# Hybrid encoder block on one core: GpSimd's share of the full stages given to VectorE, and VectorE and ScalarE ordered by due time

## The chip, the core and the metric

The kernel runs on one core of a Trainium2 chip. Five engines work side by side: PE (TensorE, matrix products), DVE (VectorE), ACT (ScalarE), POOL (GpSimd) and SP (SyncE, which here issues most DMAs). Each engine takes its own instructions in the order in which the program gives them to it, and waits on semaphores for the others. The metric is the device time of one launch in microseconds (us), lower is better.

## What is computed

One layer of an encoder with batch 1, 512 positions and width 1024, all in float32:

```
mod = silu(c) @ w_ada + b_ada                       # six vectors: shift, scale, gate for two sub-layers
h   = rms_norm(x, norm1_g) * (1 + sc1) + sh1
xr, yr, q, k, v, gates = split(h @ w_in)
branch_a = (bidir_rg_lru(depthwise_conv(xr)) * gelu(yr)) @ w_rnn_o
branch_b = diff_attention(rope(q), rope(k), v) @ w_attn_o      # 8 heads, two softmaxes each, per-head norm
x = x + g1 * ((sigmoid(ga) * branch_a + sigmoid(gb) * branch_b) @ w_out)
h = rms_norm(x, norm2_g) * (1 + sc2) + sh2
val, gt = split(depthwise_conv(h @ w_up))            # 2 x 2816 columns
x = x + g2 * ((silu(gt) * val) @ w_down)
return rms_norm(x, final_g)
```

## The kernel before

All activations lie transposed: 128 rows of the width by 512 positions, so a tile of width 1024 is eight tiles of 128x512. Every product is split for precision. An operand is held as a high part in a short format (fp32r) and a low part, the remainder, and PE makes three products of them: high by high, high by low, low by high. For every block of weights of 128x1024 (`raw`, fetched by SP) ACT casts the high part (`whi`) and then a second engine subtracts to make the low part (`wlo`, function `low`, line 468). The same pair of steps is done for activations: `mg7h` and `mg7l` are the high and low parts of the merged branches of tile 7, `qs` and `kh`/`kl` those of queries and keys, `on` those of the normalised attention output, `h2` those of the second norm.

PE's products follow one list of jobs (`ORDER`, `ORDER2` and the loops at lines 892 to 916): the gate and rnn products, then q, k and v of the attention, the second gate (`gb`), the attention's output (`ao`), the mixer's output (`op`), the feed-forward up products (`up`) and the down products (`dn`). The attention itself is a loop of 32 steps (8 heads by 4 blocks of 128 queries, line 1492): scores (`sc`), a softmax (row maxima `mx` on DVE, two exponentials `p` on ACT, the sums' reciprocal and its product with lambda, `sm`, on DVE, and the difference `p` on DVE), four transposes on PE (`pt`), the split of the transposed weights (`wth` on ACT, `wtl` on DVE) and the product with v (`po`). The jobs run between the steps.

The order on each engine is not written by hand. `build` records instructions as nodes with a cost and with what each comes after; `Program.order` (line 259) then plays a list schedule over five engines: at each point it takes the engine that can start first, and on that engine the node with the lowest number among those that are ready, that is the oldest in the recorded program. ACT adds `PATIENCE = 300` to the number of a node that would need another function table. Modulation rows (`raw<-raw,crow`, `modulation`, line 629) and weight splits stand in the same lists as the softmax.

Which engine does a piece is set by hand: `POOL_LOW` names 28 weight blocks whose low part POOL makes; `GQ`, `GK`, `GR` name the pieces of the rotary embedding (`rotary`, line 689) that POOL makes (the low parts of q and k, and the sum of the two rotated terms); the product with the sine table (`rs`, line 698) is always POOL's; of the attention's output norm (`normal`, line 1465) POOL makes the low part of every odd head, and of the second norm (`normed`, line 1575) the product of tiles 2 and 5. All of them read two tiles from on-chip memory.

Of the kernel before, what the change touches and what calls it, by code (L numbers as in the profile page):

```python
# [30 lines left out]

FETCH, AHEAD = 4, 2
HI, LO = 1, 2
POOL_LOW = (
    30, 31, 32, 34, 35, 38, 39, 40, 42, 44, 46, 47, 49, 52, 53, 55, 58, 60, 62, 64, 66, 67, 70, 73, 75, 76, 77, 78,
)

WARM = 8, 2, 5

# [4 lines left out]
CONV = 2, 2, 2  # L44
DEC, SCAN = 2, (2, 1, 1)

GQ = 1, 1, 0, 0, 1, 1, 1, 0, 1, 1, 0, 1, 0, 1, 1, 1
GK = 0, 1, 0, 0, 1, 1, 0, 1, 0, 0, 1, 1, 1, 1, 1, 0
GR = 1, 1, 1, 1, 0, 1, 1, 0, 1, 0, 1, 1, 1, 1, 0, 0
ROT = 3, 3, 2  # L50


# [13 lines left out]
UPN = 3  # L66


PATIENCE = 300


VEC = {}
# [16 lines left out]


PEQ, DVE, ACT, POOL, SPQ = range(5)

TABLES = {
    AF.Exp: (0,), AF.Sigmoid: (2,), AF.Tanh: (0, 2, 11, 18), AF.Gelu_apprx_tanh: (11,), AF.Sqrt: (3,), AF.Silu: (18,),
# [40 lines left out]
class View:  # L135
# [29 lines left out]
    def resolve(self):  # L165
        t = self.base.real
        for name, args, kwargs in self.ops:
            t = getattr(t, name)(*args, **kwargs)
        return t


class Program:
# [86 lines left out]
    def order(self):  # L259

        count = len(self.nodes)
# [14 lines left out]
        def done(n, t):  # L276
            todo = [(n, t)]
            while todo:
# [3 lines left out]
                for m in then[n]:  # L282
# [4 lines left out]
                    if not left[m]:  # L287
# [3 lines left out]
                        else:  # L291
                            heapq.heappush(waiting[f], (ready[m], m))

        for n in range(count):
            if not self.after[n]:
                if self.nodes[n][0] is None:
                    result.append(n)
                    done(n, 0.0)
                else:
                    heapq.heappush(waiting[self.nodes[n][0]], (0.0, n))  # L300
        while True:
# [11 lines left out]
                break  # L313
            t, e = best
            while waiting[e] and waiting[e][0][0] <= t:
                heapq.heappush(able[e], heapq.heappop(waiting[e])[1])
            if e == ACT:
                def rank(n):
                    kind = self.nodes[n][3]
                    load = kind[0] == "table" and kind[1] is not None and table not in kind[1]  # L320
                    return n + PATIENCE * load

                n = min(able[e], key=rank)
                able[e].remove(n)
                heapq.heapify(able[e])
            else:
                n = heapq.heappop(able[e])
            _, _, cost, kind = self.nodes[n]
            if isinstance(kind, tuple) and kind[0] == "table":
                if kind[1] is not None and table not in kind[1]:  # L330
                    cost, table = cost + 3080, kind[1][0]
            if e == DVE and kind:
                cost += 1.1 * max(0.0, min(cost, busy[POOL] - t))
            if e == POOL and busy[DVE] > t:
                cost *= 1.25
            clock[e] = busy[e] = t + cost
# [50 lines left out]
def build(nc, tc, ctx, a, out):  # L387
# [301 lines left out]
    def rotary(head, j):  # L689


        def task(ps):
# [2 lines left out]
            V.stream_shuffle(sh, ps, MASK)  # L695
            V.tensor_tensor(t, ps, cosT[j], mult)
            on_pool = GR[2 * head + j]
            G.tensor_tensor(sh, sh, sinT[j], mult)
            yield ROT[0]
            (G if on_pool else V).tensor_tensor(t, t, sh, add)  # L700
            yield ROT[1 + on_pool]
# [763 lines left out]
    def normal(j, rb, f):  # L1465
        if j not in ons:
            ons[j] = H(f"on{j}h", F32R), H(f"on{j}l", F32R)
        V.scalar_tensor_tensor(oT[j][:, f], oT[j][:, f], gsub, rb, mult, mult)
        yield 1
        A.copy(ons[j][0][:, f], oT[j][:, f])  # L1470
        yield 1
        low(ons[j][0][:, f], oT[j][:, f], ons[j][1][:, f], G if j % 2 else V)
        if f.start:
            free(oT[j])
            on[j] = ons[j]
# [99 lines left out]
    def normed(f, ss):  # L1575
# [6 lines left out]
        for k in range(NK + 2):  # L1582
            if k < NK:
                t[k] = H(f"h2f{k}{f.start}")
                (G if k % 3 == 2 else V).tensor_tensor(t[k][:, :n], x[k][:, f], rstd[:, :n], mult)
            if 1 <= k <= NK:
                u = t[k - 1][:, :n]
                A.activation(u, u, AF.Identity, bias=mod[:, 3, k - 1 : k], scale=am[:, 1, k - 1 : k])
                A.copy(h2[k - 1][0][:, f], u)
            if k >= 2:  # L1590
                low(h2[k - 2][0][:, f], t[k - 2][:, :n], h2[k - 2][1][:, f])
                free(t[k - 2])
                done2[f.start, k - 2] = True
            yield 1
# [148 lines left out]
```

## Time and profile before

| | us |
|---|---|
| median of 3 runs | 945.72 (945.37 to 947.54) |
| the profiled execution, device time | 945.66 |
| its span, first to last instruction | 943.9 |
| PE busy | 924.3 (98%) |
| DVE busy | 650.8 (69%) |
| ACT busy | 519.1 (55%) |
| POOL busy | 211.0 (22%) |

The profile is of one execution on the chip. A profile line of a group gives the operation, the tile that it writes and those that it reads, shapes, the count, the busy time, the mean duration of one, and the idle time of the engine just before. Matmuls overlap one another in the trace (each is shown for 0.39 us, with one beginning every 0.227 us), so PE can be shown as busy while it starts nothing for a short while. All instructions have the line of the recorder's `emit` (L232), so they are told apart by their tiles. The granted clock of TensorE was 0.992 of full speed over the span.

### The profile page before, as it was taken

Reading aid. Unit: us, or ns where it says so; the run is one execution under the profiler, and the core shown is the slowest. Engines: PE = TensorE matmul, PEld = TensorE weight load, DVE = VectorE, ACT = ScalarE, POOL = GpSimd, SP = SyncE. Lnnn points to the kernel's source line nnn. Section 1 sums busy time; section 2 is a strip of 40 time slices with the busy share of each in tenths; the row PEclk is TensorE's granted clock in tenths of the full one; section 3 lists DMA queues with packets and bytes.
Section 4 is the critical chain, followed back from the end, with each engine's and each line's share of the span. In section 5 each row is a group of like instructions: output and inputs, shape, how many; then the busy total and the mean of one; then the engine's idle time right before and its main releaser. Section 6 shows DMA issues by size and latency. Waiting matters only on the chain. (4 is left out here: it accounts for less than half of the span.)

```text
span 943.9 us, 12353 instructions
## 1 busy us (share of the span) xinstructions
PE 924.3 (98%) x4600; PEld 780.6 (83%) x4600; DVE 650.8 (69%) x937; ACT 519.1 (55%) x852; POOL 211.0 (22%) x177
## 2 busy tenths in 40 slices
PE   8999999999999999999999899999999999999996
PEld 6887888888889898888778689888888888888886
DVE  6999897894698889999898636575555555432224
ACT  5579999952467676587743327544444444332221
POOL 0080000040473465421132141241111111100100
PEclk8999999999999999999999999999999999999998
DMA  9854223215323134466656440144232233233302
GB/s 345 290 190 137 87 74 112 72 38 181 97 77 97 49 108 138 139 195 189 231 181 212 145 134 24 45 156 134 90 109 93 89 106 90 80 106 101 95 6 90
DMA packets 40195, 116.30 MB, mean 123 GB/s; under 512 B 5960, under 2 KB 8264, under 8 KB 40136
## 3 DMA queue, kind: packets, MB, share of 16 engines
q1 hardware_dynamic: 38696, 114.34, 37.4%
q10 hardware_dynamic: 1440, 1.18, 0.4%
q8 instruction: 36, 0.59, 0.3%
q14 instruction: 23, 0.19, 0.1%
HBM read 109.08 MB, written 2.23 MB: 118 GB/s over the span
## 5 line engine op out<-in xcount | busy, mean ns | idle before, releaser
L232 DVE TENSOR_TENSOR wlo<-raw,whi 128x1024 fp32r<-128x1024 f32 (+2 forms) x114 | 139.7, 1227 | 172.2 <-PE up L232 54.9
L232 ACT CAST whi<-raw 128x1024 fp32r<-128x1024 f32 (+2 forms) x134 | 138.0, 1030 | 175.3 <-PE up L232 56.2
L232 POOL TENSOR_TENSOR wlo<-raw,whi 128x1024 fp32r<-128x1024 f32 x28 | 70.6, 2523 | 170.5 <-PE gb L232 42.4
L232 DVE SCALAR_TENSOR_TENSOR fc<-up,vec,fc 128x511 f32<-128x511 f32 x88 | 65.4, 746 | 9.4 <-ACT fc L232 7.8
L232 POOL TENSOR_TENSOR fc<-fc,fc 128x512 f32<-128x512 f32 x22 | 28.5, 1297 | 192.1 <-ACT fc L232 192.1
L232 DVE SCALAR_TENSOR_TENSOR raw<-raw,crow 128x1024 f32<-128x1024 f32 x32 | 42.9, 1341 | 15.0 <-DMA raw<-in_w_ada 15.0
L232 ACT ACTIVATE p<-sc,mx 128x512 f32<-128x512 f32 x64 | 43.5, 685 | 15.6 <-DVE mx L232 15.3
L232 POOL TENSOR_TENSOR rs<-rs,sinT 128x512 f32<-128x512 f32 x16 | 21.4, 1339 | 136.9 <-DVE rs L232 127.0
L232 ACT ACTIVATE fc<-up,vec 128x512 f32<-128x512 f32 x44 | 34.0, 779 | 21.6 <-PE up L232 21.5
L232 ACT ACT_TABLE_LOAD x32 | 41.1, 1283 | 4.9 <-DVE fc L232 1.8
L232 DVE TENSOR_REDUCE mx<-sc 128x2 f32<-128x1024 f32 x32 | 38.8, 1215 | 5.0 <-PE sc L232 4.9
L232 ACT ACTIVATE ss<-xx 128x512 f32<-128x512 f32 (+1 forms) x19 | 10.7, 564 | 48.3 <-DVE xx L232 48.3
L232 ACT ACTIVATE fc<-fc 128x512 f32<-128x512 f32 x22 | 13.9, 632 | 42.5 <-DVE fc L232 42.5
L232 DVE SCALAR_TENSOR_TENSOR p<-p,sm,p 128x512 f32<-128x512 f32 x32 | 33.4, 1044 | 2.2 <-ACT p L232 1.9
L232 POOL TENSOR_TENSOR ss<-ss,ss 128x512 f32<-128x512 f32 x8 | 10.5, 1317 | 91.6 <-ACT ss L232 91.6
L232 ACT CAST wth<-pt 128x256 fp32r<-128x256 f32 x64 | 20.8, 378 | 16.8 <-PE pt L232 15.0
L232 ACT ACTIVATE p<-p,sm 128x512 f32<-128x512 f32 x32 | 23.4, 731 | 4.8 <-DVE sm L232 4.7
L232 DVE TENSOR_TENSOR wtl<-pt,wth 128x256 fp32r<-128x256 f32 x64 | 24.3, 414 | 1.3 <-ACT wth L232 1.3
L232 PE MATMUL sc<-kh,qs 128*128 128x512 f32 x64 | 24.9, 391 | 0.0
L232 PE MATMUL sc<-kl,qs 128*128 128x512 f32 x64 | 24.8, 392 | 0.0
L232 DVE TENSOR_TENSOR_SCAN r<-dec,i 128x512 f32<-128x512 f32 x16 | 21.5, 1344 | 0.4
L232 PE MATMUL pt<-con,p 128*128 128x128 f32 x128 | 19.3, 273 | 1.9 <-DVE wtl L232 1.9
(1542 smaller groups left out, 3054.1 us busy)
## 6 DMA issues: line engine op xcount, KB each, us to landing
raw<-in_w_up SPq DMA_DIRECT2D x40, 512.0 KB, 3.2
raw<-in_w_ada SPq DMA_DIRECT2D x32, 512.0 KB, 3.5
raw<-in_w_down SPq DMA_DIRECT2D x16, 512.0 KB, 3.5
rows<-in_w_ada SPq DMA_DIRECT2D x14, 512.0 KB, 5.3
raw<-in_w_yr SPq DMA_DIRECT2D x8, 512.0 KB, 3.4
raw<-in_w_ga SPq DMA_DIRECT2D x8, 512.0 KB, 3.3
raw<-in_w_v SPq DMA_DIRECT2D x8, 512.0 KB, 3.8
raw<-in_w_q SPq DMA_DIRECT2D x8, 512.0 KB, 3.2
```

What stands on the lines that cost most here:

```text
L232: getattr(owner, name)(*map(real, args), **{k: real(b) for k, b in kwargs.items()})
```

## The change

It has three parts.

**Engines.** `POOL_LOW` is empty, the three tables of the rotary embedding are all 0, and three lines that chose POOL name VectorE. 87 instructions move from POOL to DVE: 28 weight low parts, 16 `rs` products, 11 rotary sums, 11 low parts of q, 9 of k, 8 of the attention's output, and 4 products of the second norm. POOL keeps the tables at the beginning, the sums of squares, the feed-forward's products (`fc<-fc,fc`) and two products of the end.

**Order.** Before the list schedule runs, every node gets a due time: for a node that PE's products need, the place of the earliest such product in PE's own summed costs, less the costs on the way to it (plus 360 units for each step, and the transfer for a DMA). DVE and ACT then take the ready node with the earliest due time instead of the oldest; PE, POOL and SP still take the oldest. `PATIENCE` is 30000 and is added to ACT's due time.

**The schedule's cost of a conflict.** A DVE node that shares the memory port with POOL is no longer charged in proportion to the overlap but until POOL is done.

```diff
-POOL_LOW = (
-    30, 31, 32, 34, 35, 38, 39, 40, 42, 44, 46, 47, 49, 52, 53, 55, 58, 60, 62, 64, 66, 67, 70, 73, 75, 76, 77, 78,
-)
+POOL_LOW = ()
-GQ = 1, 1, 0, 0, 1, 1, 1, 0, 1, 1, 0, 1, 0, 1, 1, 1
...
+GQ = 0, 0, 0, 0, 0, 0, 0, 0, 0, 0, 0, 0, 0, 0, 0, 0
...
-PATIENCE = 300
+PATIENCE = 30000
...
+DUE = DVE, ACT
...
+        due, at = [0.0] * count, 0.0
+        for n in range(count):
+            due[n] = at
+            if self.nodes[n][0] == PEQ:
+                at += self.nodes[n][2]
+        for n in reversed(result_order(then)):
+            e, _, cost, kind = self.nodes[n]
+            if e == PEQ:
+                continue
+            cost = 0.0 if e is None else cost + 360
+            if isinstance(kind, tuple) and kind[0] == "dma":
+                cost += kind[1] / 165 + 4000
+            if then[n]:
+                due[n] = min(min(due[m] for m in then[n]) - cost, due[n])
...
-                heapq.heappush(able[e], heapq.heappop(waiting[e])[1])
+                n = heapq.heappop(waiting[e])[1]
+                heapq.heappush(able[e], (due[n] if e in DUE else n, n))
...
-                    return n + PATIENCE * load
+                    return d + PATIENCE * load, n
...
-                cost += 1.1 * max(0.0, min(cost, busy[POOL] - t))
+                cost += max(0.0, busy[POOL] - t - 250)
...
-            G.tensor_tensor(sh, sh, sinT[j], mult)
+            V.tensor_tensor(sh, sh, sinT[j], mult)
...
-        low(ons[j][0][:, f], oT[j][:, f], ons[j][1][:, f], G if j % 2 else V)
+        low(ons[j][0][:, f], oT[j][:, f], ons[j][1][:, f])
...
-                (G if k % 3 == 2 else V).tensor_tensor(t[k][:, :n], x[k][:, f], rstd[:, :n], mult)
+                V.tensor_tensor(t[k][:, :n], x[k][:, f], rstd[:, :n], mult)
```

`result_order` only lists the nodes so that each stands behind what it comes after.

**Place one, VectorE between the merge of tile 6 and the split of tile 7** (`gb6`, `gb7`: the gated branches, `ao`: attention's output product, `raw90`: a modulation row, `wo`, `wu`: weights of later stages, `wlo_66`, `wlo_67`: low parts of the weight blocks 66 and 67). Before:

```order
L232 SCALAR_TENSOR_TENSOR gb6_4670<-gb6_4670,ao6_5031 128x512
L232 TENSOR_TENSOR gb6_4670<-gb6_4670,ga6_1789 128x512
L232 SCALAR_TENSOR_TENSOR raw90_5175,mod_94<-raw90_5175,crow_96 128x1024
L232 TENSOR_TENSOR mg6l_4923<-gb6_4670,mg6h_4913 128x512
L232 TENSOR_TENSOR wo11l_5241<-wo1r1_4906,wo11h_5209 128x512
L232 TENSOR_TENSOR wu31l_5207<-wu3r1_5059,wu31h_5238 128x512
L232 SCALAR_TENSOR_TENSOR gb7_4690<-gb7_4690,ao7_5080 128x512
L232 TENSOR_TENSOR gb7_4690<-gb7_4690,ga7_1718 128x512
L232 SCALAR_TENSOR_TENSOR raw94_5221,mod_94<-raw94_5221,crow_96 128x1024
L232 TENSOR_TENSOR mg7l_4794<-gb7_4690,mg7h_4928 128x512
```

Changed:

```order
L249 SCALAR_TENSOR_TENSOR gb6_4664<-gb6_4664,ao6_5015 128x512
L249 TENSOR_TENSOR gb6_4664<-gb6_4664,ga6_1792 128x512
L249 TENSOR_TENSOR wlo_66_5182<-raw87_5110,whi_66_5169 128x1024
L249 TENSOR_TENSOR mg6l_4906<-gb6_4664,mg6h_4901 128x512
L249 SCALAR_TENSOR_TENSOR raw90_5167,mod_94<-raw90_5167,crow_96 128x1024
L249 TENSOR_TENSOR wlo_67_5243<-raw89_5142,whi_67_5217 128x1024
L249 SCALAR_TENSOR_TENSOR gb7_4680<-gb7_4680,ao7_5057 128x512
L249 TENSOR_TENSOR gb7_4680<-gb7_4680,ga7_1728 128x512
L249 TENSOR_TENSOR wu11l_3897<-wu1r1_4811,wu11h_3686 128x512
L249 TENSOR_TENSOR wo01l_4954<-wo0r1_4813,wo01h_4938 128x512
L249 TENSOR_TENSOR mg7l_4796<-gb7_4680,mg7h_4910 128x512
```

Two weight low parts come in from POOL ahead of `gb7`, two splits for later stages (`wo11l`, `wu31l`) go behind it; PE's products around `op` and ACT's casts around `mg7h` stand as before.

**Place two, VectorE in the attention's loop, head 3** (`rs30`, `rt30`, `qs30`, `qs31`: the rotated query and its low parts; `rs30<-rs30,sinT0` and `rt30<-rt30,rs30` stood on POOL before). Before:

```order
L232 TENSOR_REDUCE mx22_2657<-sc22_2790 128x2
L232 STREAM_SHUFFLE rs30_2706<-pq3_2798 128x512
L232 TENSOR_TENSOR rt30_2695<-pq3_2798,cosT0_103 128x512
L232 RECIPROCAL sm22_2713<-sm22_2713 128x2
L232 TENSOR_TENSOR sm22_2713<-sm22_2713,nlam_102 128x1
L232 TENSOR_TENSOR wtl120_2625<-pt13_2883,wth120_2627 128x2x128
L232 TENSOR_TENSOR wtl121_2623<-pt13_2883,wth121_2620 128x2x128
L232 SCALAR_TENSOR_TENSOR p220_2682<-p221_2778,sm22_2713,p220_2682 128x512
L232 TENSOR_REDUCE mx23_2700<-sc23_2853 128x2
L232 TENSOR_TENSOR qs31_2704<-rt30_2695,qs31_2704 64x512
```

Changed:

```order
L249 STREAM_SHUFFLE rs30_2722<-pq3_2820 128x512
L249 TENSOR_TENSOR rt30_2709<-pq3_2820,cosT0_103 128x512
L249 TENSOR_TENSOR rs30_2722<-rs30_2722,sinT0_105 128x512
L249 RECIPROCAL sm22_2700<-sm22_2700 128x2
L249 TENSOR_TENSOR sm22_2700<-sm22_2700,nlam_102 128x1
L249 TENSOR_TENSOR wtl120_2625<-pt13_2885,wth120_2627 128x2x128
L249 TENSOR_TENSOR wtl121_2619<-pt13_2885,wth121_2615 128x2x128
L249 SCALAR_TENSOR_TENSOR p220_2705<-p221_2789,sm22_2700,p220_2705 128x512
L249 TENSOR_TENSOR rt30_2709<-rt30_2709,rs30_2722 128x512
L249 TENSOR_TENSOR wlo_38_2811<-raw38_2601,whi_38_2815 128x1024
L249 TENSOR_REDUCE mx23_2753<-sc23_2873 128x2
L249 TENSOR_TENSOR qs30_2707<-rt30_2709,qs30_2707 64x512
```

Between the maxima of blocks 2 and 3 DVE now also holds the sine product, the rotary sum and the low part of weight block 38.

**Place three, ScalarE at the very end** (`ss37`: squares of the last tile, which PE sums for the final norm; `xg7`: the same tile scaled for the output; `rn30`, `rn31`: the roots of the two halves). Before:

```order
L232 ACTIVATE rn30_7451<-ss30_7825 128x256
L232 DMA out_0_dram<-xg1_7392 128x256
L232 DMA out_0_dram<-xg3_7411 128x256
L232 DMA out_0_dram<-xg5_7420 128x256
L232 DMA out_0_dram<-xg7_7423 128x256
L232 ACTIVATE ss37_7427<-xx7_5064 128x256
L232 ACTIVATE xg7_7423<-xx7_5064,vec_83 128x256
L232 ACTIVATE rn31_7453<-ss3256_8176 128x256
```

Changed:

```order
L249 ACTIVATE rn30_7451<-ss30_7825 128x256
L249 DMA out_0_dram<-xg1_7392 128x256
L249 DMA out_0_dram<-xg5_7420 128x256
L249 DMA out_0_dram<-xg3_7411 128x256
L249 DMA out_0_dram<-xg7_7423 128x256
L249 ACTIVATE xg7_7423<-xx7_5284,vec_83 128x256
L249 ACTIVATE ss37_7427<-xx7_5284 128x256
L249 ACTIVATE rn31_7453<-ss3256_8180 128x256
```

The scaling of the last tile now stands ahead of its squares.

## Rows read from the trace of the kernel before

**Rows 1.** The page's first part: busy time, share and instructions of each engine.

```profile
PE 924.3 (98%) x4600; PEld 780.6 (83%) x4600; DVE 650.8 (69%) x937; ACT 519.1 (55%) x852; POOL 211.0 (22%) x177
```

**Rows 2.** Waits of PE: who waited for whom, total us, times, longest us.

```profile
PE op L232 <- ACT mg7h L232: 4.0, 1, 4.0
PE pt L232 <- DVE wtl L232: 1.9, 4, 0.9
...
PE ao L232 <- ACT on1h L232: 0.8, 1, 0.8
```

**Rows 3.** Timeline of VectorE, 505 to 532 us: start us, us, instruction, idle before.

```profile
514.74 2.88 DVE L232 TENSOR_TENSOR mg5l<-gb,mg5h 128x512 fp32r<-128x512 f32 x1
...
522.35 2.73 DVE L232 TENSOR_TENSOR wu31l<-wu3r,wu31h 128x512 fp32r<-128x512 f32 x1
525.00 0.67 DVE L232 SCALAR_TENSOR_TENSOR gb<-gb,ao 128x512 f32<-128x512 f32 x1
525.70 0.69 DVE L232 TENSOR_TENSOR gb<-gb,ga 128x512 f32<-128x512 f32 x1
```

**Rows 4.** Timeline of GpSimd at the same place.

```profile
521.88 2.65 POOL L232 TENSOR_TENSOR wlo<-raw,whi 128x1024 fp32r<-128x1024 f32 x1 [4.80 <-ACT whi L232]
```

**Rows 5.** Timeline of PE, 520 to 545 us.

```profile
519.79 0.39 PE L232 MATMUL op<-mg1h,whi 128*128 128x512 f32 x1
...
523.19 0.39 PE L232 MATMUL op<-mg1l,whi 128*128 128x512 f32 x1
```

**Rows 6.** Busy time by stretch: PE, PEld, DVE, ACT, POOL, granted clock, DMA share, GB/s.

```profile
235.00:525.00 290.00, 285.52 (x1564) 243.68 (x1563) 251.79 (x399) 183.19 (x377) 116.66 (x72) 1.00 0.46 144
...
528.60:532.00 3.40, 3.40 (x9) 2.65 (x9) 0.67 (x3) 1.04 (x1) 0.00 (x0) 0.50 0.41 146
```

**Rows 7.** GpSimd by operation and shape, 235 to 525 us.

```profile
L232 POOL TENSOR_TENSOR wlo<-raw,whi 128x1024 fp32r<-128x1024 f32 x22 | 54.6, 2484 | 146.7 <-PE gb L232 42.4 <-ACT whi L232 31.7 <-issue 24.7
L232 POOL TENSOR_TENSOR rs<-rs,sinT 128x512 f32<-128x512 f32 x14 | 18.6, 1325 | 14.2 <-DVE rs L232 12.0 <-DVE sm L232 2.0
L232 POOL TENSOR_TENSOR rt<-rt,rs 128x512 f32<-128x512 f32 x9 | 13.4, 1492 | 0.7
L232 POOL TENSOR_TENSOR qs<-rt,qs 64x512 fp32r<-64x512 f32 x9 | 12.3, 1367 | 9.5 <-ACT qs L232 7.3 <-PE po L232 1.9
L232 POOL TENSOR_TENSOR kl<-rt,kh 64x512 fp32r<-64x512 f32 x8 | 10.3, 1289 | 14.8 <-ACT kh L232 9.6 <-DVE kl L232 5.0
```

**Rows 8.** VectorE by operation and shape, 235 to 525 us.

```profile
L232 DVE SCALAR_TENSOR_TENSOR p<-p,sm,p 128x512 f32<-128x512 f32 x32 | 33.4, 1044 | 2.2 <-ACT p L232 1.9
...
L232 DVE TENSOR_TENSOR wlo<-raw,whi 128x1024 fp32r<-128x1024 f32 x16 | 21.1, 1318 | 1.9 <-ACT p L232 1.0 <-ACT whi L232 0.5 <-issue 0.4
L232 DVE TENSOR_TENSOR sm<-sm,nlam 128x1 f32<-128x1 f32 x32 | 18.6, 581 | 1.1
L232 DVE TENSOR_TENSOR gb<-gb,ga 128x512 f32<-128x512 f32 x7 | 8.3, 1191 | 0.2
...
L232 DVE TENSOR_TENSOR qs<-rt,qs 64x512 fp32r<-64x512 f32 x5 | 7.0, 1398 | 2.7 <-ACT qs L232 2.5
...
L232 DVE TENSOR_TENSOR kl<-rt,kh 64x512 fp32r<-64x512 f32 x6 | 4.1, 683 | 1.0 <-ACT kh L232 0.9
...
L232 DVE TENSOR_TENSOR on4l<-oT,on4h 128x256 fp32r<-128x256 f32 x2 | 0.8, 412 | 0.0
```

**Rows 9.** Single tiles, 235 to 530 us: duration ns min/median/max, first and last start.

```profile
L232 DVE TENSOR_TENSOR sm<-sm,nlam x32: 158/160/2164, 244.3 to 447.9; 128x1 f32<-128x1 f32 x32
L232 DVE SCALAR_TENSOR_TENSOR p<-p,sm,p x32: 734/752/2415, 245.1 to 450.1; 128x512 f32<-128x512 f32 x32
...
L232 DVE TENSOR_TENSOR wlo<-raw,whi x16: 1211/1218/2173, 254.5 to 509.8; 128x1024 fp32r<-128x1024 f32 x16
```

**Rows 10.** Timeline of ScalarE at the end, 933 to 944 us.

```profile
935.02 0.42 ACT L232 ACTIVATE ss<-xx 128x256 f32<-128x256 f32 x1 [6.40 <-DVE xx L232]
935.35 0.49 ACT L232 ACTIVATE xg<-xx,vec 128x256 f32<-128x256 f32 x1
```

More of the change, by code (lines that the diff above doesn't have):

```diff
@@ L45 @@
 DEC, SCAN = 2, (2, 1, 1)
-GQ = 1, 1, 0, 0, 1, 1, 1, 0, 1, 1, 0, 1, 0, 1, 1, 1
-GK = 0, 1, 0, 0, 1, 1, 0, 1, 0, 0, 1, 1, 1, 1, 1, 0
-GR = 1, 1, 1, 1, 0, 1, 1, 0, 1, 0, 1, 1, 1, 1, 0, 0
+GQ = 0, 0, 0, 0, 0, 0, 0, 0, 0, 0, 0, 0, 0, 0, 0, 0
+GK = 0, 0, 0, 0, 0, 0, 0, 0, 0, 0, 0, 0, 0, 0, 0, 0
+GR = 0, 0, 0, 0, 0, 0, 0, 0, 0, 0, 0, 0, 0, 0, 0, 0
 ROT = 3, 3, 2
@@ L169, in resolve, with result_order @@
         return t
+def result_order(then):
+    left = [0] * len(then)
+    for b in then:
+        for m in b:
+            left[m] += 1
+    todo, result = deque(n for n, k in enumerate(left) if not k), []
+    while todo:
+        n = todo.popleft()
+        result.append(n)
+        for m in then[n]:
+            left[m] -= 1
+            if not left[m]:
+                todo.append(m)
+    return result
 class Program:
@@ L315, in order, with rank @@
             while waiting[e] and waiting[e][0][0] <= t:
-                heapq.heappush(able[e], heapq.heappop(waiting[e])[1])
+                n = heapq.heappop(waiting[e])[1]
+                heapq.heappush(able[e], (due[n] if e in DUE else n, n))
             if e == ACT:
-                def rank(n):
+                def rank(entry):
+                    d, n = entry
                     kind = self.nodes[n][3]
                     load = kind[0] == "table" and kind[1] is not None and table not in kind[1]
-                    return n + PATIENCE * load
-                n = min(able[e], key=rank)
-                able[e].remove(n)
+                    return d + PATIENCE * load, n
+                entry = min(able[e], key=rank)
+                able[e].remove(entry)
                 heapq.heapify(able[e])
+                n = entry[1]
             else:
-                n = heapq.heappop(able[e])
+                n = heapq.heappop(able[e])[1]
             _, _, cost, kind = self.nodes[n]
```

## The prediction

> **What bounds the kernel.** I read the page's busy times first: PE is busy for 924.3 of 943.9 us [rows 1], so the most that any change of the other engines can return is what PE loses in waits and at a lowered clock. The second view is PE's list of waits [rows 2]. It is short. One wait of 4.0 us stands before the first product of the mixer's output that needs `mg7h`; four waits in the attention's loop, 1.9 us together, are for `wtl`; one of 0.8 us is for the attention's output norm. The third view is the busy time by stretch [rows 6], in which the granted clock is the last but two of the columns. Right behind the long wait, from 528.6 to 532.0, it is 0.50, the lower of the two levels (1.2 GHz): PE had stood idle for the 4.0 us before. Nine products lie in these 3.40 us. At the full clock a product begins every 0.227 us (16 from 519.79 to 523.19, 3.40 us by 15 steps, [rows 5]), so nine are worth 2.04 us, and the lowered clock costs 1.4 us. The wait and its clock together are 5.4 us, more than all else that PE waits for in the full stages.
>
> Why did PE wait for `mg7h`? The timeline of VectorE [rows 3] tells it. The merge of tile 7 (`gb`) began only at 525.00, though its product had ended before 519.79, where PE was already in the next job. Ahead of it in VectorE's order stood `wu31l`, a weight split that is needed far later, and that took 2.73 us where a subtraction of that shape takes 0.69 (the `gb` sum right behind it). GpSimd was at a weight low part from 521.88 to 524.53 [rows 4], and `wu31l` ended 0.6 us after that: it stood still until GpSimd was done. `mg5l` lost 2.2 us in the same way [rows 3]. The group means against medians [rows 8, 9] show that this is common: `sm<-sm,nlam`, one column, takes 0.160 us at the median, 0.581 in the mean and 2.164 at most.
>
> **The change, part by part.** The stretch from 235 to 525 us (attention, its norm, both projections) holds 70 of the 87 moved instructions. VectorE is busy there for 251.8 of 290.0 us and idle for 38.2 [rows 6].
>
> *Added to VectorE there.* 22 weight low parts at 1.218 (median, [rows 9]), 26.8 us. 40 rotary pieces (14 `rs`, 9 `rt`, 9 `qs`, 8 `kl`, [rows 7]) at the 0.683 that VectorE's own `kl` takes [rows 8], 27.3 us. 8 low parts of the norm at 0.412 [rows 8], 3.3 us. Sum 57.4 us.
>
> *Returned to VectorE there*, since no GpSimd instruction that reads memory is left beside it: `sm` 32 times 0.581 less 0.160, 13.5 us; `p` 32 times 1.044 less 0.752, 9.3; the `gb` sums 7 times 1.191 less 0.69, 3.5; `qs` 5 times 1.398 less 0.683, 3.6; `wlo` 16 times 1.318 less 1.218, 1.6; `mg5l` and `wu31l` 2.2 and 2.0 [rows 3, 8, 9]. Sum 35.7 us. If the long durations had another cause, nothing returns; that is the lower bound. I take 35.7, because the blocked instructions end where GpSimd's end. VectorE then needs 251.8 + 57.4 - 35.7 = 273.5 of 290 us, and 16.5 are left idle instead of 38.2. With nothing returned it would need 309.2, which is 19.2 more than there is.
>
> *The wait for `mg7h`.* In the changed order six instructions lie from the merge of tile 6 up to the merge of tile 7 (place one): two of 0.67 and 0.69, `mg6l` 0.69, and three of 1,024 columns at 1.22, together 5.7 us. PE needs 24 products for one `ao` tile, 24 times 0.227 = 5.4 us, so VectorE about keeps pace, and the merge of tile 7 should begin at most one such instruction, 1.2 us, after its product ends. Before, `wu31l` alone took 2.73 us there, and the merge of tile 6 was late already because of `mg5l` [rows 3]. After the merge come its sum and ACT's cast, for which I take the 0.69 of VectorE on the same shape: 1.2 + 0.67 + 0.69 + 0.69 = 3.3 us. PE has 18 products of `op` to do meanwhile, 4.1 us. So the wait should fall from 4.0 to near nothing; bounds are 0 and 4.0, I take 0.3 for handoffs. Without the wait the clock has no cause to fall: the 1.4 us return (bounds 0 and 1.4). Gain 3.7 + 1.4 = 5.1 us.
>
> *The attention's waits.* Now 1.9 + 0.8 = 2.7 us [rows 2]. Due-first takes `wtl` ahead of older work that nobody needs yet, and the blocks are gone, but VectorE has less idle time to make good a late one. Bounds are 0 and, with 32 steps each a little late, some 5 us more than now; I take 0.5 us of gain, nearest to the row as it is.
>
> *The end.* ACT now scales the last tile before it squares it (place three). Before, that scaling of 0.49 us ran beside PE's sum [rows 10]; now it lies ahead of it on the path to the end. Cost 0.4 us (0.33 to 0.49).
>
> *The rest costs nothing.* 17 moved instructions lie in stages where VectorE has idle time, at the first projections' end, in the second norm and at the beginning of the feed-forward; PE covers them. Two function-table loads fall away in ACT's new order, and ACT is no bound there (183.2 of 290 us busy, [rows 6]). SP's DMAs follow the release of the same buffers; a weight block is released about a microsecond earlier when VectorE makes its low part (1.2 instead of 2.5 us), and modulation rows stand in gaps of VectorE. What SP's order moves I hold to be covered by PE's work; if a block lands late it shows as a wait of VectorE and is in the bounds above.
>
> Sum against the profiled execution's own 945.66 us (the median of the runs, 945.72, is the same): 945.66 - 5.1 - 0.5 + 0.4 = 940.5 us.
>
> **A rule that speaks against the change.** The Trainium skill, page "Perfetto Trace Analysis", section "Optimizing Scalar/DVE Operations", advises the opposite: where VectorE is saturated, offloading to ScalarE or even GpSimd may make sense. Taken alone, it would have the 57.4 us come on top, and the time rise as in rival 2 below, at its worse end. The same skill, page "SBUF — State Buffer", section "Who interferes with whom", says that a VectorE instruction with two on-chip inputs and a GpSimd instruction that reads on-chip memory exclude each other for the whole instruction; by it the 35.7 us return. The trace sides with the second: the maxima of rows 9, and `mg5l` at 2.88 us.
>
> **The rivals.**
>
> 1. *The wait moves, the time does not.* The wait for `mg7h` goes, but VectorE, with 16.5 us of idle time left, is a little late in each of the attention's 32 steps. At 0.15 us each that is 4.8 us: 945.66 - 5.1 + 0.4 + 4.8 = 945.8. For it: the moved pieces lie where VectorE is fullest. Against it: the late pieces have the first place in the new order, and weight low parts and modulation rows, which can be late without harm, fill the rest.
>
> 2. *VectorE becomes the bound from 235 to 525 us; slower.* The idle 38.2 us are waits of an engine that works in order: for ACT's exponentials, PE's scores, landed blocks. Whatever of them cannot be filled must fit in the 16.5 us. From the point where more than 16.5 us of them stay, each further one delays PE. If two thirds stay, 25.5 us, PE ends 9.0 us later, and the time is 945.66 - 5.1 + 0.4 + 9.0 = 950.0. If none of the blocked time came back it would be worse by up to 19.2 us. For it: the waits are named by the trace. Against it: PE now waits for VectorE only 1.9 us in the loop although the blocks hit it at random, so there is room between a piece and its use.
>
> 3. *The wait for `mg7h` stays in part.* A modulation row (`raw90`) and a weight block (`wlo_67`) stand ahead of the merge of tile 7 and need a landed DMA or a free buffer. If one is 2 us late, 2 us of wait and perhaps the clock's 1.4 us stay: 942.5 to 943.9.
>
> **How the numbers follow.** A measurement of this kernel can tell about 0.3%, 2.8 us, from no change. My forecast has 0.55, rival 1 0.17, rival 2 0.13 and rival 3 0.15, about half of it below 942.9. Faster by over 0.3% is the forecast and that half, 0.63; within 0.3% are rival 1 and the other half, 0.24; slower is rival 2, 0.13. The low end of the range has the whole wait, its clock and all 2.7 us of the other waits gone, 945.66 - 8.1 + 0.4 = 938.0, and one more for short delays between products that the list of waits leaves out: 937.0. The high end takes in rival 1 and the milder half of rival 2: 948.0.
>
> **What would show it right or wrong.** Right: in the changed profile the list of PE's waits has no `op <- mg7h` above 1 us and no stretch at clock 0.50 near 530 us; the median and the mean of `sm<-sm,nlam` agree at 0.16; the VectorE is busy for about 273 us in the same stretch; the last tile's `xg` stands before its `ss`. Wrong: PE's waits for `wtl`, `qs`, `kl` or `vs` sum to more than 5 us between 235 and 476 us (rivals 1 and 2), `sm` keeps maxima of 2 us (the block had another cause), or the wait for `mg7h` stands with a DMA or `wlo` before it (rival 3).

## The result, and the profile after

The changed kernel takes 936.71 us (median, 935.71 to 938.64); the kernel before, run beside it, 946.63 (945.37 to 949.69). The ratio is 0.9893, 95% interval 0.9863 to 0.9923: faster by 1.1%. The forecast was 940.5 with a range from 937.0: right in direction and kind, too small in size, and the time lies 0.3 us under the range. The profiled execution took 936.87 us (span 935.1); before, 945.66 (span 943.9). So 8.8 us have to be found.

The page's busy line of the changed kernel, for [rows 1]:

```profile
PE 918.5 (98%) x4600; PEld 776.7 (83%) x4600; DVE 658.9 (70%) x1024; ACT 518.3 (55%) x850; POOL 66.2 (7%) x90
```

PE's list of waits in the changed kernel, for [rows 2]:

```profile
PE xrw L249 <- DVE zeros L249: 1.5, 1, 1.5
PE xrw L249 <- ACT h1h L249: 1.3, 1, 1.3
PE pq L249 <- DVE vs10l L249: 1.0, 1, 1.0
PE ss L249 <- ACT ss L249: 1.0, 1, 1.0
...
PE ao L249 <- ACT on0h L249: 0.5, 1, 0.5
```

The 4.0 us for `mg7h` and the 1.9 us for `wtl` are gone. The first two lines lie in the first 100 us; `vs10l` is the low part of a tile of v. Busy time by stretch (columns as in [rows 6]; the granted clock stands behind GpSimd's column):

```profile
235.00:525.00 290.00, 287.94 (x1580) 245.98 (x1580) 262.79 (x472) 184.02 (x379) 1.05 (x2) 1.00 0.46 146
525.00:560.00 35.00, 35.00 (x196) 30.76 (x195) 19.25 (x30) 11.38 (x16) 5.58 (x4) 1.00 0.43 145
528.60:532.00 3.40, 3.40 (x16) 2.82 (x15) 2.20 (x5) 1.15 (x2) 0.00 (x0) 1.00 0.40 137
```

VectorE took over 70 pieces in the first stretch and is busy for 11 us more only (262.8 against 251.8). The last row is the same stretch of time that ran at half the clock before: 16 products now, where nine were. Groups of VectorE from 235 to 525 us, for [rows 8, 9]:

```profile
L249 DVE TENSOR_TENSOR wlo<-raw,whi 128x1024 fp32r<-128x1024 f32 x39 | 47.4, 1218 | 7.3 <-ACT whi L249 7.2
...
L249 DVE SCALAR_TENSOR_TENSOR p<-p,sm,p 128x512 f32<-128x512 f32 x32 | 24.0, 749 | 3.8 <-ACT p L249 3.5
L249 DVE TENSOR_TENSOR qs<-rt,qs 64x512 fp32r<-64x512 f32 x14 | 9.6, 686 | 0.7 <-ACT qs L249 0.2
...
L249 DVE TENSOR_TENSOR gb<-gb,ga 128x512 f32<-128x512 f32 x8 | 5.5, 692 | 0.3
...
L249 DVE TENSOR_TENSOR sm<-sm,nlam 128x1 f32<-128x1 f32 x32 | 5.1, 160 | 1.1
```

Every mean shown now stands at the former median, or at what VectorE took for that shape alone. VectorE's timeline around the merge of tile 7 (start, duration, both in us), for [rows 3]:

```profile
516.51 1.22 DVE L249 TENSOR_TENSOR wlo<-raw,whi 128x1024 fp32r<-128x1024 f32 x1
517.65 0.68 DVE L249 SCALAR_TENSOR_TENSOR gb<-gb,ao 128x512 f32<-128x512 f32 x1
518.36 0.69 DVE L249 TENSOR_TENSOR gb<-gb,ga 128x512 f32<-128x512 f32 x1
```

The merge begins at 517.65 instead of 525.00, and no instruction is longer than its kind takes alone.

**Where the 8.8 us came from.** The list of waits leaves out delays of a few tenths, so I add up, over all 4,600 products of a trace, the distance from one start to the next less the usual distance of that shape (0.2265 us for 512 columns, 0.1189 for 256; the 166 narrower products likewise, and the value taken for them moves the columns almost alike). The totals differ from kernel to kernel as the spans do.

| us lost by PE in | before | after | lows_moved_alone | lows_moved_old_plan | rotary_back |
|---|---|---|---|---|---|
| 0 to 100 (start) | 11.28 | 10.15 | 11.01 | 10.60 | 10.96 |
| 100 to 250 | 0.44 | 0.50 | 0.51 | 1.62 | 0.51 |
| 250 to 450 (attention) | 7.45 | 6.87 | 5.57 | 7.94 | 5.09 |
| 450 to 500 (its norm, first `ao`) | 3.37 | 1.60 | 2.23 | 3.91 | 1.09 |
| 500 to 550 (`ao`, `mg7h`, `op`) | 5.99 | 0.50 | 0.72 | 1.53 | 1.13 |
| 550 to 600 | 2.01 | 1.82 | 2.03 | 2.02 | 1.81 |
| 600 to the end | 2.01 | 2.32 | 1.99 | 2.01 | 2.31 |
| sum | 32.56 | 23.74 | 24.06 | 29.62 | 22.90 |

From before to after: 5.5 us at `mg7h`, 1.8 in the attention's norm, 0.6 in its loop, 1.1 at the start, 0.1 elsewhere, less 0.3 at the end. (The last three columns are experiments below. Each column is one profiled execution.)

### The profile page after: what moved, and what is told of

Read it like the earlier page. It is cut to its first block, busy times and chain, and to the rows that moved or that the text cites. A ratio compares the mean times of both kernels' runs of the same rounds, so it can differ in the third digit from the quotient of the medians.

```text
span 935.1 us, 12263 instructions
## 1 busy us (share of the span) xinstructions
PE 918.5 (98%) x4600; PEld 776.7 (83%) x4600; DVE 658.9 (70%) x1024; ACT 518.3 (55%) x850; POOL 66.2 (7%) x90
## 3 DMA queue, kind: packets, MB, share of 16 engines
HBM read 109.08 MB, written 2.23 MB: 119 GB/s over the span
## 5 line engine op out<-in xcount | busy, mean ns | idle before, releaser
L249 DVE TENSOR_TENSOR wlo<-raw,whi 128x1024 fp32r<-128x1024 f32 (+2 forms) x142 | 170.4, 1201 | 177.2 <-PE up L249 57.7
L249 DVE SCALAR_TENSOR_TENSOR raw<-raw,crow 128x1024 f32<-128x1024 f32 x32 | 39.5, 1235 | 13.7 <-DMA raw<-in_w_ada 13.5
L249 DVE SCALAR_TENSOR_TENSOR p<-p,sm,p 128x512 f32<-128x512 f32 x32 | 24.0, 749 | 3.8 <-ACT p L249 3.5
L249 DVE TENSOR_TENSOR_SCAN r<-dec,i 128x512 f32<-128x512 f32 x16 | 18.7, 1209 | 0.0
L249 PEld LDWEIGHTS pt<-con,p 128*128 128x128 f32 x128 | 15.5, 140 | 3.4 <-issue 0.3
```

Source lines behind the costliest of these rows:

```text
L249: getattr(owner, name)(*map(real, args), **{k: real(b) for k, b in kwargs.items()})
```

## The experiments

Each ratio is to runs of the kernel before on the same chip, and times are medians; those medians of before were 946.2 to 948.1, so runs on different chips are better compared by their ratios. The theory at the outset (A) was the prediction's: GpSimd's reads hold VectorE up, and the change ends that. The third part of the change, the planner's price of a conflict, was not run by itself: engines_only and order_only both keep the changed price.

### The change cut in two: engines or order

**engines_only.** The changed kernel with `DUE = ()` and `PATIENCE = 300`.

> The changed kernel with the old order on VectorE and ScalarE (oldest in the program first, a table load put off by 300), so only the engines of the 87 pieces are changed. Theory A (the gain is the end of VectorE's blocks behind GpSimd's reads; the order adds a part): about 940.5 us (938.5 to 942.5), VectorE busy in 235 to 525 us for some 263 us as in the changed kernel (262.8), sm mean 0.16 us, the wait for mg7h below 1.5 us; about 4 us above the changed kernel. Rival B (the order by due time makes the gain, the engines cost): 945 to 952 us, with the wait for mg7h and others kept or larger. Rival C (the engines are all of it): 936.7 us within 1.

Measured: 937.78 us, ratio 0.9902 (0.9876 to 0.9927). 1.1 us above the changed kernel where A expected 4, which the runs hardly tell from nothing: rival C is nearest. VectorE is busy for 261.57 us from 235 to 525 us, and the wait for `mg7h` is 0.7 us.

**order_only.** The changed kernel with `POOL_LOW`, the three tables and the three `G` lines put back.

> The changed kernel with all 87 pieces back on GpSimd, but with due-first order on VectorE and ScalarE and the changed cost of a shared port in the planner. Theory A: the blocks stay (sm mean about 0.5 us, VectorE 250 us busy in the stretch), and only some late pieces are mended by the order: 943 us (940.5 to 945.5). Rival B: about 936 to 938 us, no wait above 1 us. Rival C: 945 to 948 us, the order alone brings nothing.

Measured: 944.65, ratio 0.998 (0.9967 to 0.9992); `sm` 0.394 us in the mean, the `gb` sums 1.383. The order, with the changed price in it, is worth some 2 us. B falls. What the order would give with the former price was not run; lows_back_old_cost below shows that the price can matter by far more than 2 us.

The wait for `mg7h` is gone here too, though all blocks are left (PE loses nothing from 500 to 550 us, 6.0 before). In its place stands a wait in the attention's norm, for `oT`, the attention's output before its norm,

```profile
PE rb L251 <- DVE oT L251: 2.2, 1, 2.2
```

with a granted clock of 0.50 right behind it (475 to 480 us). So a single long wait can be moved by the order alone; that it is gone does not show a gain.

### GpSimd's reads put back, nothing else

**ghost_reads** and **ghost_writes.** A scratch tile, and at the former places

```diff
+    def beside(n):
...
+        G.tensor_tensor(ghost_[:, :n], crow[:, :n], crow[:, :n], add)
```

or, for the second, memsets of the same tile. The planner leaves them out of every cost and due time.

> The changed kernel, the same instructions in the same order on PE, VectorE, ScalarE and SyncE, and beside them, at 83 of the 87 places (all but the second norm's), an addition on GpSimd of the former width (28 of 1,024 columns, 47 of 512, 8 of 256) that reads a constant row twice and writes a scratch tile nobody reads. VectorE's own work is unchanged, so any time lost is GpSimd's doing. Theory A: reads on GpSimd block VectorE again: sm mean back to 0.4 or more, maxima of 1.3 us and more, VectorE busy in 235 to 525 us for 285 us or more (262.8 plus a good half of the 46 us that came back), and PE waits: 950 us (942 to 965). Rival (the long VectorE instructions had another cause, as the accesses of the split weights themselves): 936.7 within 1.5, sm mean 0.16.

> As the one before, but GpSimd only writes there: memsets of 1,024 columns of bfloat16 of the scratch tile (four, two or one in a row for a piece of 1,024, 512 or 256 columns), nothing read. Theory A, with the block tied to reads: the time of the changed kernel, 936.7 within 1.5, sm mean 0.16 and VectorE 263 us in the stretch. Rival (any GpSimd access to on-chip memory blocks or slows VectorE): above 940 us, with long sm as in the run with reads, in proportion to GpSimd's busy time.

Measured: with reads 992.48, ratio 1.0489 (1.0457 to 1.052); with writes 937.95, ratio 0.9904 (0.9879 to 0.9929). The edit missed its aim in one respect: nothing tied the additions to their places, and 60 of the 83 ran one after the other from 74 to 176 us (the memsets likewise, from 73 to 223 us). That makes the stretch from 100 to 175 us a measurement of its own, with the same program on VectorE in three kernels. Busy times there, with reads and then with writes:

```profile
100.00:175.00 75.00, 50.05 (x195) 39.93 (x195) 74.90 (x47) 32.14 (x47) 71.62 (x44) 0.80 0.16 54
```

```profile
100.00:175.00 75.00, 75.00 (x377) 64.00 (x377) 68.23 (x91) 71.48 (x105) 70.93 (x72) 1.00 0.24 78
```

GpSimd is as busy in the one as in the other. With reads VectorE gets through 47 instructions in place of 91 while shown busy all the time. Its groups from 75 to 180 us in the changed kernel, with reads, and with writes:

```profile
L249 DVE TENSOR_TENSOR i<-i,th 128x512 f32<-128x512 f32 x12 | 7.7, 682 | 1.4 <-ACT th L249 1.4
L249 DVE COPY gl<-yr 128x512 f32<-128x512 f32 x8 | 5.5, 684 | 0.7 <-PE yr L249 0.7
L249 DVE CAST whi<-raw 128x1024 fp32r<-128x1024 f32 x7 | 4.8, 688 | 1.6 <-PE ga L249 1.3 <-PE yr L249 0.3
```

```profile
L254 DVE TENSOR_TENSOR i<-i,th 128x512 f32<-128x512 f32 x6 | 9.7, 1654 | 0.0
L254 DVE CAST whi<-raw 128x1024 fp32r<-128x1024 f32 x4 | 6.1, 1526 | 0.0
L254 DVE COPY gl<-yr 128x512 f32<-128x512 f32 x7 | 4.7, 678 | 0.0
```

```profile
L254 DVE TENSOR_TENSOR i<-i,th 128x512 f32<-128x512 f32 x12 | 7.7, 682 | 1.1 <-ACT th L254 1.1
L254 DVE CAST whi<-raw 128x1024 fp32r<-128x1024 f32 x7 | 6.4, 908 | 1.4 <-PE ga L254 1.1 <-PE yr L254 0.3
L254 DVE COPY gl<-yr 128x512 f32<-128x512 f32 x8 | 5.5, 684 | 0.7 <-PE yr L254 0.7
```

A product of two tiles in on-chip memory takes 0.682 us alone and beside writes, 1.654 beside reads; a copy out of PE's accumulators 0.68 in all three. So the block itself is shown: reads, not writes, against instructions with two on-chip inputs. This is what the Trainium skill says ("SBUF — State Buffer", section "Who interferes with whom"), and the trace agrees.

**ghosts_in_place.** As ghost_reads, but each addition waits for VectorE's piece:

```diff
+        G.tensor_tensor(mark_[rows], piece, crow[rows, :1], add)
...
+        G.tensor_tensor(ghost_[:, :n], crow[:, :n], crow[:, :n], add)
```

> The changed kernel, same instructions in the same order on PE, VectorE, ScalarE and SyncE. In the first run with added reads nothing tied the 83 additions to their places: GpSimd ran them one after the other until about 180 us. Here each waits, by a read of one column, for the piece that VectorE now does at its place, so they are spread as the pieces were before. Theory A: from 235 to 525 us VectorE gets back the blocked time, about 46 us if the blocks are as frequent as before, and needs some 300 us of 290: sm mean 0.4 us or more, PE waits of 5 to 20 us, time 947 us (941 to 957). Rival (the reads did harm only because they came without a gap; pieces with gaps cost VectorE nothing that PE sees): 936.7 within 1.5, with sm mean up to 0.3.

Measured: 969.51, ratio 1.023 (1.0215 to 1.0246), above even the expected range. PE's waits, with VectorE's order as in the changed kernel:

```profile
PE pt L254 <- DVE wtl L254: 6.7, 7, 2.0
PE op L254 <- ACT mg7h L254: 6.4, 1, 6.4
PE sc L254 <- DVE qs L254: 3.9, 2, 3.5
```

The two longest waits of [rows 2] are back and larger. `sm` takes 0.415 us in the mean, as A expected; VectorE is busy for 272.9 of the 290 us, not for 300, since it gets through only 434 of its 472 instructions there. An order that was planned without the blocks loses some 32 us to them (1.023 against 0.9893).

### Which of the 87 pieces

**lows_back, rotary_back.** The changed kernel with `POOL_LOW` as before; the changed kernel with `GQ`, `GK`, `GR` and the sine product as before.

> The changed kernel with only the 28 weight low parts back on GpSimd (new order kept). All 87 back cost 944.65 - 936.71 = 7.9 us. If the loss goes with GpSimd's time, the low parts have 22 x 2.48 = 55 of its 117 us in the stretch and cost about 3.8 us: 940.5 (939 to 942). Rival 1 (the long instructions, up to 2.65 us, are what hurts): 943 to 945. Rival 2 (low parts have slack and the rotary pieces hurt): 936.5 to 938.

> The changed kernel with only the rotary pieces (rs, rt, qs, kl) back on GpSimd. By GpSimd's time (about 56 of 117 us): 940.5 (939 to 942). Rival 1 (the long low parts hurt): 936.5 to 938. Rival 2 (the rotary pieces hurt, since PE's scores wait for them and GpSimd needs twice as long for each): 943 to 945.

Measured: lows_back 959.43, ratio 1.0126 (1.0098 to 1.0154); rotary_back 935.28, ratio 0.9867 (0.985 to 0.9883). All that was expected falls, for both. The rotary pieces gain nothing on VectorE that the runs can tell. And rotary_back still has blocks:

```profile
L249 DVE SCALAR_TENSOR_TENSOR p<-p,sm,p 128x512 f32<-128x512 f32 x32 | 26.7, 835 | 6.5 <-ACT p L249 5.5 <-issue 0.6
L249 DVE TENSOR_TENSOR sm<-sm,nlam 128x1 f32<-128x1 f32 x32 | 13.2, 414 | 1.1
```

`sm` stands at 0.414 us in the mean, as in ghosts_in_place, and PE loses less than in the changed kernel. VectorE is busy for 255.8 us from 235 to 525 us against 262.8: the blocks take less from it than the rotary pieces would. So blocks need not cost PE anything; I conclude that they cost where PE waits for what stands behind them. That lows_back is worse than order_only (944.65), which has even more pieces on GpSimd, needed a cause of its own: the next run but one. It is not a lack of time on VectorE, which is less busy there than in the changed kernel (columns as in [rows 6]):

```profile
235.00:525.00 290.00, 274.34 (x1491) 231.80 (x1490) 246.75 (x420) 175.41 (x367) 53.29 (x22) 0.99 0.40 127
```

**lows_halves.** lows_back, each low part on GpSimd as two subtractions of 512 columns; every engine's order unchanged.

```diff
...
+        for u in (slice(0, half), slice(half, 2 * half)):
+            self.owner.tensor_tensor(out[:, u], a[:, u], b[:, u], op)
```

> lows_back (959.4 us) with each of the 28 low parts on GpSimd cut into two subtractions of 512 columns, one behind the other; every engine's order is the same. GpSimd reads as long in all (28 x 2 x about 1.3 us against 28 x 2.5), but VectorE can come in between. If the length of one block makes the loss: about 948 us (943 to 953), with sm's maximum near 1.3 us instead of over 2. If GpSimd's reading time as a whole makes it, or the lateness of the low part itself: 958 to 962.

Measured: 957.13, ratio 1.0109 (1.0093 to 1.0125). The blocks did get shorter (the longest `sm` 1.136 us, in lows_back 2.170), but that was worth at most 2.3 us of the 22.7, and the two intervals overlap.

**lows_back_old_cost.** lows_back with one line of the planner as before.

```diff
-                cost += max(0.0, busy[POOL] - t - 250)
+                cost += 1.1 * max(0.0, min(cost, busy[POOL] - t))
```

> lows_back with the planner's former cost of a shared port (1.1 times the overlap, up to the instruction's own length, in place of what is left beyond 250). If lows_back is slow because the planner, with the changed cost, puts VectorE's pieces at the wrong times: 944 to 950. If it is slow because VectorE, with the rotary work, is held up by GpSimd's long reads whatever the order: 956 to 962.

Measured: 942.96, ratio 0.9954 (0.994 to 0.9969). Some 16 us come from the planner's price of a block and no moved instruction: between 250 and 450 us PE loses 21.6 us in lows_back and 6.8 here. The longest of PE's waits from 235 to 450 us, in lows_back and in this kernel:

```profile
PE v L251 <- DVE rt L251: 4.6, 2, 2.4
PE pq L251 <- DVE vs20l L251: 1.9, 1, 1.9
PE sc L251 <- ACT p L251: 1.8, 2, 1.1
```

```profile
PE sc L251 <- DVE qs L251: 0.8, 1, 0.8
PE pq L251 <- DVE sm L251: 0.3, 1, 0.3
```

Which of the planner's choices did this was not followed further. The wait for `mg7h`, gone in lows_back, is back here at 2.5 us.

**due_vector_only.** The changed kernel with `DUE = (DVE,)` and `PATIENCE = 300`.

> The changed kernel with the due-first order on VectorE alone; ScalarE takes the oldest first, a table load put off by 300, as before. The order as a whole is worth 1.1 us (937.78 without it). Theory: ScalarE's share is the casts of the attention's output norm (a wait of 3.7 us less 1.5 in the stretch 450 to 475 us stands in the run without the new order): without it the wait for on0h is back at 1 us, 937.5 (936.5 to 938.5), and xg comes after ss at the end. Rival (VectorE's order makes it all): 936.7 or less, since the last tile's sum is no longer late: 936.0 to 936.7.

Measured: 937.01, ratio 0.9887 (0.9873 to 0.9902), the same as the changed kernel. The expected wait for `on0h` did not come; 450 to 500 us lose 0.9 us where engines_only loses 3.8, so it is VectorE's order that mends that stretch.

### One part alone, in the kernel before

**lows_moved_alone.** The kernel before with `POOL_LOW = ()` and nothing else.

> The kernel before with one edit: the 28 weight low parts go to VectorE; rotary pieces and norms stay on GpSimd, order and planner's costs as before. Theory D (formed from lows_back and rotary_back: the low parts are the whole gain, since a GpSimd read of 2.5 us holds up a chain of VectorE's short pieces that a later product needs; the rotary pieces, 1.3 us each, are not worth moving): 936 to 939.5 us, ratio about 0.989, the wait for mg7h below 1.5 us. Rival E (the due-first order or the planner's changed cost is needed for it, and each half of the change alone loses): 943 us or more.

Measured: 937.39, ratio 0.9903 (0.9888 to 0.9918). One line gives 9 of the 10 us, with the rule of the order and the costs of before; the orders themselves are planned anew, on PE and ScalarE too. The time is D's, and E falls. D's cause is tested by the next runs.

**late_lows_moved, early_lows_moved.** Only the 12 low parts from 464 us on, or only the 16 before, move; the first line is what stays on GpSimd in late_lows_moved, the second what stays in early_lows_moved.

```diff
+POOL_LOW = 30, 31, 32, 34, 35, 38, 39, 40, 42, 44, 46, 47, 49, 52, 53, 55
...
+POOL_LOW = 58, 60, 62, 64, 66, 67, 70, 73, 75, 76, 77, 78
```

> The kernel before with 12 of the 28 low parts moved to VectorE, those that began at 464 us and later (58 to 78); the 16 of the attention's loop stay on GpSimd. If the gain is made in the norm and the projections: the excess of PE from 450 to 560 us falls from 9.5 to about 3, 940.5 (939 to 942). If it is made in the attention's loop: 943.5 to 946.

> The other half: the 16 low parts of 235 to 450 us move to VectorE, the 12 later ones stay. If the gain is made late: 944 (942.5 to 946), with the wait for mg7h still there at 2 us or more. If in the attention's loop: 938 to 941.5. The two halves' gains should add up to the 9.5 us of lows_moved_alone, unless each half is worth nothing while the other blocks.

Measured: late 938.37, ratio 0.991 (0.9892 to 0.9927); early 940.15, ratio 0.9927 (0.9906 to 0.9949). The late half gains 8.0 us, more than expected; the early half 6.2, where 944 was expected if the gain is made late. So neither place has it all, and as the halves together give 9.5, each mends part of what the other does (I take it that a late chain can be mended ahead of its long block or at it; no run shows that by itself, and each edit also makes a new plan). The late half cannot be told from all 28 (0.991 against 0.9903, with intervals that overlap). In the late one PE loses 0.4 us from 500 to 550 us (5.99 before) and 2.1 from 450 to 500, while the waits for `wtl` stay at 1.9 us. In the early one `wu31l` still stands behind GpSimd (2.76 us), but the merge of tile 7 begins 2 us earlier (523.05), and 1.6 us of the wait for `mg7h` are left.

**lows_moved_ghosts.** lows_moved_alone with 28 additions of 1,024 columns, each after a low part, which the planner counts.

> lows_moved_alone (937.39) with 28 additions on GpSimd, each of 1,024 columns, each after the low part that VectorE now does; they read a constant row twice and write a tile nobody reads, and the planner counts them as it counted the low parts. If the long reads beside VectorE are what costs: 947 (944 to 956), since VectorE has the low parts and the blocks as well. If it is the low parts being ready sooner, or their buffers released sooner: 937 to 939.

Measured: 947.05, ratio 1.0006 (0.9993 to 1.0019): the whole gain is gone. The cause is not as clean as the number. 3.4 us are a wait for `rhh`, the high part of the attention norm's roots, whose cast stands on ScalarE behind another that waited 3.42 us for a weight's DMA, and that is a matter of the new order. Of the 10.6 us that PE loses more than in lows_moved_alone, 8.2 lie in 450 to 500 us around that wait (the granted clock is 0.50 from 480 to 485 us, behind it), 3.9 in the attention.

**lows_moved_old_plan.** The kernel before with the 28 low parts issued on VectorE and planned as GpSimd's; no order changes on any other engine.

```diff
+    planned_on_pool = Recorder(program, POOL, nc.vector)
...
-            low(hi, raw, lo, G if i in POOL_LOW else V)
+            low(hi, raw, lo, planned_on_pool if i in POOL_LOW else V)
```

> The kernel before with the 28 low parts issued on VectorE, but planned as if they still ran on GpSimd: PE, ScalarE, SyncE and what is left of GpSimd keep the order of before instruction for instruction, and VectorE's order is that of before with the 28 put in where the planner had them. If the reads beside VectorE are what costs, the move gives its gain without any new order: 938.5 (936.5 to 941), sm's mean down from 0.58 to about 0.45, gb sums at 0.69, and the wait for mg7h below 1.5 us. If the gain comes from the new plan: 944 to 950, as VectorE now has 27 us more in an order made without them.

Measured: 942.87, ratio 0.9963 (0.9943 to 0.9984), between the two. VectorE's timeline at the place of [rows 3], in the same order with `wlo` put in:

```profile
521.94 0.69 DVE L232 TENSOR_TENSOR wu31l<-wu3r,wu31h 128x512 fp32r<-128x512 f32 x1
522.55 1.22 DVE L232 TENSOR_TENSOR wlo<-raw,whi 128x1024 fp32r<-128x1024 f32 x1
523.68 0.68 DVE L232 SCALAR_TENSOR_TENSOR gb<-gb,ao 128x512 f32<-128x512 f32 x1
```

`wu31l` takes 0.69 us where it took 2.73, with nothing changed but the engine of the low parts. Two of PE's waits:

```profile
PE op L232 <- ACT mg7h L232: 1.2, 1, 1.2
...
PE lamps L232 <- DVE ga L232: 1.1, 1, 1.1
```

The wait for `mg7h` falls from 4.0 to 1.2 us, and 500 to 550 us lose 1.5 us instead of 6.0. The attention and its norm lose somewhat more than before (7.9 and 3.9, where 7.5 and 3.4 were lost). So the engine alone mends most of the wait for `mg7h`, and the 5.5 us from here to lows_moved_alone come from the new plan in which the low part is VectorE's own work. That plan also reorders PE and ScalarE. And 1.1 of the 5.5 us only take back the second wait shown, at 241 us, which the kernel before does not have: the old order had no place for more work on VectorE. The other way round, the new plan with the low parts still on GpSimd, was not run, so the split of 3.3 and 5.5 us holds for this sequence of the two steps.

### A better version

**low_parts_due_vector.** The changed kernel with the rotary pieces on GpSimd, `DUE = (DVE,)` and `PATIENCE = 300`.

> The version that the runs point to: the changed kernel with the rotary pieces left on GpSimd and the due-first order on VectorE alone (ScalarE as before). From rotary_back (935.28) and due_vector_only (937.01 against 936.71 with both): 935.2 (934 to 936.5), the last wait for the output norm's sum (ss) at 0.6 instead of 1.0 us; faster than the changed kernel by 0.1 to 0.2%. Rival (the two add nothing to one another): 936.7 or above.

Measured: 934.78 us (934.38 to 935.97), ratio 0.9876 (0.9861 to 0.9891). The wait for `ss` is 0.6 us, as expected. It is the fastest by its median, 1.9 us under the changed kernel, but the ratio of rotary_back, on another chip, is lower (0.9867). The intervals of all three overlap, so a lead over the changed kernel is likely and not shown, and a lead over rotary_back is not even likely.

## Why the prediction was right and wrong

*The wait for `mg7h` and its clock (5.1 us).* Right in place, cause and size: 5.5 us. lows_moved_old_plan shows the cause alone: 4.5 of the 6.0 us lost from 500 to 550 us go with the low parts' engine. It is not the only way to that end, as order_only has no such wait either. No `op <- mg7h` above 1 us is left, and the clock is 1.00 from 505 to 535 us.

*VectorE's sum (273.5 us).* Measured 262.8: 46.4 came back (251.8 + 57.4 - 262.8) where 35.7 were listed. The list was made from groups with a mean far from the median and left out those with a few long ones: the modulation rows (1.314 us before, 1.218 now, some 24 of them) give 2.3 us, and one `mod` sum of 2.290 us, an `osqs` split of 1.678 and the two `rh` steps some 4 us more; the rest I did not itemize, and the window holds slightly different work now. Means at the medians and `sm` at 0.160 came as said. But the step that was drawn from this sum, VectorE's idle time as the measure of danger, was beside the point: lows_back has more of it (290 - 246.8 = 43.2 us) than the changed kernel (27.2), and takes 23 us longer.

*The attention's waits (0.5 us).* This is the step that failed: the term is too small. The prediction had 2.7 us of listed waits there and took 0.5 of them, because VectorE would have less idle time to make good a late piece. In the changed kernel the loop and the norm gained 2.4 us (0.6 and 1.8), in lows_moved_alone 3.0, in rotary_back 4.6. The listed waits of that stretch fell by 1.1 us: `wtl`, 1.9, and `on1h`, 0.8, are gone; `on0h` is at 0.5 instead of 0.2, and 1.3 for `vs10l` and `vs20l` came in. The other 1.3 us are delays too short for the list, for which only the low end of the range had a microsecond. Why they fell is shown in part. In lows_moved_old_plan, without the low parts' blocks but in the old order, the attention and its norm gain nothing; with the new plan of lows_moved_alone they gain. So the gain there hangs on what the planner makes of the moved pieces, which the prediction did not price. That it puts a low part where VectorE is idle, and moves up what PE needs, is my reading; no row shows it, and for the changed kernel itself, with its order by due time, engine and plan were not taken apart.

*The rest at nothing.* The start gained 1.1 us in the profiled execution. Kernels whose first 120 rows on PE, VectorE and ScalarE are those of before lose from 10.5 to 12.4 us there in their single profiles, so much of these 1.1 us may be scatter. The granted clock from 10 to 30 us is 0.83 before and 1.00 after, but it is 1.00 in lows_moved_old_plan too, whose first instructions are those of before, and 0.82 to 0.83 in lows_moved_alone: no moved piece sets it. Together with the attention's 1.9 us beyond the 0.5 and the 0.4 at `mg7h` they make 3.4 of the 3.6 us between the 5.2 of the sum and the 8.8 of the profile. That the time lies under the range, and not just inside it, is a matter of 0.3 us, less than the runs of one kernel differ.

*The end (+0.4 us).* Right: `xg` stands before `ss` on ScalarE,

```profile
925.81 0.51 ACT L249 ACTIVATE xg<-xx,vec 128x256 f32<-128x256 f32 x1 [6.32 <-DVE xx L249]
926.23 0.40 ACT L249 ACTIVATE ss<-xx 128x256 f32<-128x256 f32 x1
```

and PE's wait for it is 1.0 us; it was 0.6 before and is 0.6 in due_vector_only.

*The rivals.* None came in the change itself: VectorE had 27 us left, and neither a DMA nor `wlo` held `mg7h`. Something like rival 2 is seen in ghosts_in_place, where the blocks stay beside all of VectorE's work. lows_back is as slow as rival 2 and more, but not by its mechanism: VectorE has time left, and the planner's former price gives most of the loss back. Offloading from a full VectorE was weighed as a rule against the change, for all 87 pieces at once. For the low parts the runs go against it by 9 us; for the rotary pieces they do not: 935.28 with them on GpSimd, 936.71 without. The prediction read only half of what the Trainium skill says there ("Perfetto Trace Analysis", "Optimizing Scalar/DVE Operations"): the next sentence has it that GpSimd and VectorE share a read port, so that offloading between the two might not help. The low parts agree with that sentence; the rotary pieces neither help nor harm.

## What to carry to other kernels

When two engines share a port, don't add up the blocked time; look for what stands behind each block and whether the bounding engine waits for it, and try the kinds of moved work one by one, for here one of three carried the gain and one gave nothing (the third, the norms' pieces, was not run by itself). Where a planner sets the order, moving a piece has two effects, the engine's and the new plan's, and the second can be the larger: price it by issuing the piece on the new engine in the old order, as lows_moved_old_plan does. A planner's price of a conflict can be as strong a lever as the engine (some 16 us between lows_back and lows_back_old_cost), so it must be tried again whenever the work that conflicts changes.

## What the runs showed of the hardware that I had not expected

VectorE's cast of a weight block (`whi<-raw`, one on-chip input, 0.688 us for 1,024 columns) is slowed by GpSimd's writes too: 0.908 us beside memsets, 1.526 beside reads, while instructions with two on-chip inputs of 512 columns stay at 0.682 beside writes. The Trainium skill ("SBUF — State Buffer", section "Who interferes with whom") says that casts can use both port pairs, and can then contend with GpSimd; the rows agree. 207 us of GpSimd writes cost the kernel nothing that the runs can tell (937.95 against 936.71), 143 us of reads, most of them without a gap, cost 56 (992.48).
